# Eight half-MiB loads more, a branch on all counts, and free banks for the last scatter

## The chip, the cores and the metric

The kernel runs on one core of a Trainium2 chip. The metric is device time in microseconds (us), the median of several executions. A profile was taken of one more execution; all times of single instructions come from it, counted from the start of its span.

## The reference

A trunk of two layers on 256 tokens of width 1024. Each layer has a mixer (a gated delta rule and a sparse attention) and a feed-forward part: the first layer's is dense, the second's has eight experts, of which every token goes to two. What the change touches is the second one:

```python
def moe_ffn(h, w_router, w1, w3, w2):
    logits = (h @ w_router).astype(jnp.float32)
    top_val, top_idx = lax.top_k(logits, TOP_K)
    top_w = jax.nn.softmax(top_val, -1)
    combine = jnp.sum(jax.nn.one_hot(top_idx, N_EXPERTS, dtype=jnp.float32) * top_w[..., None], -2)
    out = jnp.zeros_like(h)
    for e in range(N_EXPERTS):
        out = out + combine[..., e:e + 1].astype(h.dtype) * swiglu(h, w1[e], w3[e], w2[e])
    return out
```

All is fp32. An expert's w1 and w3 are 1024 x 3584, its w2 is 3584 x 1024: 42 MiB an expert, 336 MiB for the eight.

## The kernel before

**Router.** After the second mixer the logits `lg` are ranked on VectorE (DVE), `sel` marks each token's two experts, and TensorE (PE) sums `sel` into the bank `pk` (line 1145): places of the tokens in their experts and, in columns 16 to 23, the number of tokens of each expert. `cnt0` (1151) is expert 0's count as an integer; `slot` (1153) is each token's place.

**Large and small experts.** An expert is computed by `Large` with 128 slots for tokens, or by `Small` with 64. `Large` splits each weight block into two parts of fp32r, hi on ScalarE (ACT) and lo on DVE (`split`, 216; rows of it stand under lines 233 and 235), and multiplies three times. The parts' tiles are `hi` and `lo` of the pool `spl` (three each) and `hi2` and `lo2` of the stage's own pool (one each), of 1072 columns. `Small` multiplies the fp32 blocks as they are, without parts, two 64-column halves side by side. Both run four groups of columns (`GRP`): `up` for w1 and w3, `mid` for silu and the transposes, `down` for w2 into the bank `py`, and at the end `scatter`, which brings the result back to the tokens and adds it to `acc` (1360).

**Gather.** `gathered` (1156) multiplies tokens with a one-hot matrix of the slots into one bank `pg`; eight DVE instructions (1165) take two such banks out. Banks named by `mi` come from the pair with the tag `pj`, which `pk`, `pg`, `put`, `pot` and `pso` share. A bank passes on to a new name when the last instruction that uses the old one is done. `hidden` (1139) hands out the four banks of the tags `dn` and `no`.

**Loads.** Weights come in 1 MiB loads, issued by SP (SyncE) in `fetch` (1214), into a ring of 14 tiles that earlier stages have used (1347). Before the branch the first 14 loads of expert 0 are issued (`loaded`, 1389 to 1395); `blocks` (1206) takes those first and then fetches further ones, each when its ring tile has been read.

**Order and branch.** From the router to `manual.close()` (1387) PE and DVE run in the order of the code. The planner orders the rest. Then every engine loads `cnt0` into a register (1493) and branches (1494): with over 64 tokens for expert 0 it runs `experts(False, ...)`, else `experts(True, ...)`. In `experts` expert 0 comes first, the others sorted by count so that large and small ones alternate: seven places, of which those from `SMALL` = 4 on are small. In the branch of 64 slots the order is small, large, small, large, large, small, large, small. `rest` works out this order, the weights and `gf2`.

**After the branch**, every engine loads `cnti`, the greatest count (of the small ones, 64 more), and branches (1501, 1502): over 128, a loop over all experts computes the tokens that found no slot, and stores the result again. `store` (1367) writes `acc`, four blocks of 256 KB: those of the first 128 tokens from ACT's queue, of the others from SP's.

Of the kernel before, what the change touches and what calls it, by code (L numbers as in the profile page):

```python
# [16 lines left out]
P = 128  # L17
# [69 lines left out]
def trunk(ctx, tc, A, out, dbg=None, stop=None):  # L87
# [39 lines left out]
    def bc(ap, shape):  # L127
        return ap.to_broadcast(shape)
# [973 lines left out]
    def moe(mp, lg, rf, px, am, manual):  # L1102
# [7 lines left out]
        eq = T([P, NT, 8, 8], "eq", bufs=2, tag="u")  # L1110
        own, other = bc(lg[:, :, :, None], [P, NT, 8, 8]), bc(lg[:, :, None, :], [P, NT, 8, 8])
# [27 lines left out]
        def hidden():  # L1139

            seq["ph"] = seq.get("ph", -1) + 1
            return bank(("dn", "dn", "dn", "no")[seq["ph"] % 4], "ph")
# [8 lines left out]
        cnt0 = T([P, 1], "cnt0", I32)  # L1151
        V.tensor_copy(cnt0, pk[:, 16:17])
# [53 lines left out]
        def blocks(w, e, r0, n, c0, width, get):  # L1206

            per = 2048 // width
            for i in range(0, n, per):
                r = loaded.pop(0) if loaded else fetch(w, e, r0 + i * P, per, c0, width, get)  # L1210
                for j in range(per):
                    yield r[:, j]

        def fetch(w, e, a, per, c0, width, get):
            r = get().rearrange("p (k n) -> p k n", k=per)
            nc.sync.dma_start(r, w[bass.ds(e, 1), a:a + per * P, c0:c0 + width].rearrange("e (k p) n -> p (e k) n", p=P))
            return r
# [66 lines left out]
        class Small:  # L1284
# [44 lines left out]
            def scatter(self, t, onet, fin):  # L1329
# [4 lines left out]
                po = [mi("pso") for n in range(2)]  # L1334
# [32 lines left out]
        def store(t, d):  # L1367
            (nc.sync if t else nc.scalar).dma_start(o_[:, t, d], acc[:, t, d])
# [9 lines left out]
        cp = T([P, NT, 7], "cp")  # L1378
        cnt = T([P, 8], "cnt")
        oneh = one_hot(slot[:, :, 0])  # L1380
# [5 lines left out]
        V.tensor_copy(cnt, pk[:, 16:24])  # L1386
# [69 lines left out]
        def experts(first, PLACE):  # L1456

            kinds = [first] + [place >= SMALL for place in PLACE]
            oneh = one_hot(slot[:, :, 0], first)
# [29 lines left out]
            for n in range(2):  # L1489
                prev.scatter(n, onet, add_to(weight(NE - 1), store))  # L1490

        was, had = dict(seq), list(loaded)
        few0 = nc.values_load(cnt0[0:1, 0:1], min_val=0, max_val=S)
        with tc.If(few0 > 64) as branch:
            experts(False, (4, 0, 1, 5, 2, 3, 6))
        with branch.Else():
            seq.update(was)
            loaded[:] = had
            experts(True, (0, 4, 1, 2, 5, 3, 6))

        mx = nc.values_load(cnti[0:1, 0:1], min_val=0, max_val=S + 64)
        with tc.If(mx > P):
            with tc.For_i(0, NE, 1) as ev:
                es_ = T([P, NT], "es")
                ec = T([P, NT], "ec")
                V.tensor_copy(es_, late_[:, :, bass.ds(ev, 1)].rearrange("p t o -> p (t o)"))
                V.tensor_copy(ec, comb[:, :, bass.ds(ev, 1)].rearrange("p t o -> p (t o)"))
                oneh = one_hot(es_)
                g = gather(oneh)
                onet = turned(oneh)  # L1510
                ex = Large(ev, g, lambda: raws.tile([P, 2048], F32, tag="raw", name="ro", bufs=RAWS))
                for q in range(4):
                    ex.up(q)
                    ex.mid(q)
                    ex.down(q)
                for n in range(2):
                    ex.scatter(n, onet, add_to(lambda t: ec[:, t:t + 1]))
            for n in range(2):
                for t in range(NT):
                    store(t, slice(n * 512, n * 512 + 512))  # L1520
# [133 lines left out]
```

## Time and profile before

| | us |
|---|---|
| median of 3 runs | 1749.4 |
| lowest and highest run | 1748.41, 1754.7 |
| the profiled execution | 1749.47 |
| its span | 1747.5 |

| engine | busy us | share of the span |
|---|---|---|
| PE, matmuls | 1659.9 | 95% |
| PEld, weight loads of PE | 1290.0 | 74% |
| DVE | 1164.2 | 67% |
| ACT | 831.7 | 48% |
| POOL | 56.9 | 3% |

The chain of work that ended last is PE for 85% of the span, DMA for 6%, DVE for 5%. Matmuls are pipelined, so that a busy PE is not PE at its peak, and an average over the span mixes stages with different limits. The stage with the eight experts runs from about 882 us to the end; its rows are to be read by themselves.

### The profile page before, as it was taken

What the parts mean: (1) busy time and instruction counts of PE and PEld (TensorE: products, weight loads), DVE (VectorE), ACT (ScalarE), POOL (GpSimd) and SP (SyncE); (2) the same over time, 40 slices, a digit from 0 to 9 for tenths busy, and PEclk for the clock granted to TensorE, in tenths of its full rate; (3) what the DMA queues carried; (4) which work ended last, traced back from release to release, by engine and by line L of the source; (5) the groups of instructions that cost most, each with busy time, mean ns of one, the idle gap of its engine ahead of it and who ended that gap; (6) DMA issues with size and microseconds to landing.
All of it is one profiled execution on the core that took longest, in us unless ns stands there. A gap on an engine that the chain in (4) does not pass through costs nothing.

```text
span 1747.5 us, 28930 instructions
## 1 busy us (share of the span) xinstructions
PE 1659.9 (95%) x11230; PEld 1290.0 (74%) x11230; DVE 1164.2 (67%) x2106; ACT 831.7 (48%) x1240; POOL 56.9 (3%) x112
## 2 busy tenths in 40 slices
PE   6997999899999999899999999999999999999997
PEld 4896878899999898788844688347887873478732
DVE  6769857799996677855521888118899971288611
ACT  3664544444444565554410676007777750277500
POOL 4400000100000200000100000000000000000000
PEclk8898979999999899999999999999999999999999
DMA  9564535599985334235679999999999999999997
GB/s 338 160 207 161 178 74 209 202 359 323 329 306 165 109 120 149 80 92 217 237 294 403 409 405 407 409 403 409 404 407 405 377 349 394 403 409 403 409 408 270
DMA packets 206431, 515.22 MB, mean 295 GB/s; under 512 B 18926, under 2 KB 58422, under 8 KB 206278
## 3 DMA queue, kind: packets, MB, share of 16 engines
q1 hardware_dynamic: 196870, 509.25, 78.2%
q10 hardware_dynamic: 9312, 3.90, 0.9%
q8 instruction: 92, 1.51, 0.3%
q14 instruction: 61, 0.50, 0.1%
q0 software_dynamic: 96, 0.07, 0.0%
HBM read 512.13 MB, written 1.05 MB: 294 GB/s over the span
## 4 chain that ended last, share of the span: by engine, by line
PE 85%; DMA 6%; DVE 5%; ACT 2%; issue 1%; SPq 0%; ACTq 0%; DVEq 0%
PE ph L1236 17%; PE ph L1299 10%; PE py L1267 9%; PE pj L239 8%; PE pj L240 8%; PE pj L241 8%; DMA m<-in_w_moe_dram 4%; PE py L1326 3%; PE py L241 2%; PE py L239 2%; PE py L240 2%; PE pSs L893 1%; PE put L125 1%; PE pn L370 1%; DMA xT<-in_w_moe_dram 1%
## 5 line engine op out<-in xcount | busy, mean ns | idle before, releaser
L235 DVE TENSOR_TENSOR wml<-m,wmh 128x1024 fp32r<-128x1024 f32 (+1 forms) x240 | 248.7, 1079 | 26.9 <-ACT wmh L233 15.5
L233 ACT ACTIVATE wmh<-m 128x1024 fp32r<-128x1024 f32 (+1 forms) x240 | 218.4, 944 | 56.2 <-DMA m<-in_w_moe_dram 20.3
L1309 DVE TENSOR_TENSOR u<-u,ph 128x512 f32<-128x512 f32 (+1 forms) x16 | 9.9, 621 | 208.4 <-PE ph L1299 208.4
L1236 PE MATMUL ph<-wmh,gh 128*128 128x512 f32 x448 | 145.4, 394 | 2.2 <-ACT wmh L233 2.2
L1236 PE MATMUL ph<-wml,gh 128*128 128x512 f32 x448 | 145.9, 396 | 1.1 <-DVE wml L235 1.0
L1236 PE MATMUL ph<-wmh,gl 128*128 128x512 f32 x448 | 145.4, 394 | 0.0
L1299 PE MATMUL ph<-m,gs 128*64 128x512 f32 (+1 forms) x720 | 139.5, 538 | 2.1 <-DMA m<-in_w_moe_dram 2.1
L239 PE MATMUL pj<-hf0h,wh 128*128 128x256 f32 x448 | 126.5, 284 | 1.2 <-ACT hf0h L341 1.2
L240 PE MATMUL pj<-hf0l,wh 128*128 128x256 f32 x448 | 126.2, 283 | 0.0
L241 PE MATMUL pj<-hf0h,wl 128*128 128x256 f32 x448 | 125.2, 283 | 0.0
L233 ACT ACTIVATE w2h<-m 128x1024 fp32r<-128x1024 f32 x104 | 107.9, 1057 | 34.8 <-PE py L1267 23.2
L235 DVE TENSOR_TENSOR w2l<-m,w2h 128x1024 fp32r<-128x1024 f32 x104 | 121.9, 1220 | 2.6 <-ACT w2h L233 2.5
L1267 PE MATMUL py<-w2h,uu 128*128 128x512 f32 x448 | 121.8, 393 | 0.0
L260 DVE SCALAR_TENSOR_TENSOR adacc<-ada,cact,adacc 128x512 f32<-128x512 f32 x158 | 117.1, 757 | 3.1 <-DMA ada<-in_w_ada_dram 2.2
L1299 PEld LDWEIGHTS ph<-m,gs 128*64 128x64 f32 x720 | 50.3, 137 | 83.3 <-issue 69.9
L233 ACT ACTIVATE wh<-win 128x1024 fp32r<-128x1024 f32 x64 | 67.4, 1057 | 78.0 <-PE pj L240 60.7
L233 ACT ACTIVATE wh<-w 128x1024 fp32r<-128x1024 f32 x56 | 59.4, 1061 | 94.4 <-PE pj L240 57.9
L1236 PEld LDWEIGHTS ph<-wml,gh 128*128 128x128 f32 x448 | 82.7, 188 | 28.0 <-DVE wml L235 7.6
L1236 PEld LDWEIGHTS ph<-wmh,gh 128*128 128x128 f32 x448 | 83.8, 188 | 24.2 <-ACT wmh L233 4.8
L1267 PEld LDWEIGHTS py<-w2h,uu 128*128 128x128 f32 x448 | 84.2, 188 | 19.6
L1236 PEld LDWEIGHTS ph<-wmh,gl 128*128 128x128 f32 x448 | 84.0, 188 | 19.5
L1326 PE MATMUL py<-m,us 128*64 128x512 f32 x416 | 94.9, 597 | 1.5 <-DMA m<-in_w_moe_dram 1.5
(650 smaller groups left out, 3939.5 us busy)
## 6 DMA issues: line engine op xcount, KB each, us to landing
m<-in_w_moe_dram SPq DMA_DIRECT2D x312, 1024.0 KB, 17.4
ada<-in_w_ada_dram SPq DMA_DIRECT2D x48, 1024.0 KB, 7.6
w<-in_w_dense_dram SPq DMA_DIRECT2D x42, 1024.0 KB, 6.8
win<-in_w_in_dram SPq DMA_DIRECT2D x34, 1024.0 KB, 5.2
xT<-in_w_moe_dram SPq DMA_DIRECT2D x24, 1024.0 KB, 17.5
wout<-in_w_out_dram SPq DMA_DIRECT2D x8, 1024.0 KB, 6.3
win<-in_w_in_dram SPq DMA_DIRECT2D x8, 536.0 KB, 3.7
win<-in_w_in_dram SPq DMA_DIRECT2D x8, 528.0 KB, 3.6
```

Source lines behind the costliest of these rows:

```text
L125: return nc.tensor.transpose(out_, in_, ident[:k, :k])
L233: SC.activation(hi, src, AF.Copy)
L235: cur["last"] = eng.tensor_tensor(lo, src, hi.bitcast(F32), op=OP.subtract).ins
L239: mm(o, w[0], x[0], start=start, stop=False, skip_group_check=True)
L240: mm(o, w[0], x[1], start=False, stop=False, skip_group_check=True)
L241: mm(o, w[1], x[0], start=False, stop=stop, skip_group_check=True)
L260: V.scalar_tensor_tensor(acc, w(k), cact[:, k:k + 1], acc, op0=OP.mult, op1=OP.add)
L370: mm(o, x[0][:, kt, s], hi[:, k], start=kt == 0, stop=False)
L1236: mm(p_, s_[:, k], d_[:, i * 512:i * 512 + 512], start=k == 0 and d_ is hi and s_ is gh, stop=k == KT - 1 and d_ is lo)
L1267: mm(p_, s_[:, j], d_[:, n * 512:n * 512 + 512], start=q + j == 0 and d_ is hi and s_ is uh, stop=q == 3 and j == nb - 1 and d_ is lo)
L1299: mm(p_[i * 64:i * 64 + 64, 0:h], self.g[k], raw[:, i * h:i * h + h], start=k == 0, stop=k == KT - 1, skip_group_check=True)
L1326: mm(self.py[n * 64:n * 64 + 64], self.u[q][:, b, i * 64:i * 64 + 64], raw[:, n * 512:n * 512 + 512], start=q + j == 0, stop=q == 3 and j ...
```

## The change

- After `before`'s constants a row `most` is set on POOL: 64 for expert 0, 128 for the others. `cnt0` goes. Between `one_hot` and the first `gathered`, DVE copies the counts out of `pk` (`cnt`, before at line 1386), and with five more instructions makes `need`: 8 for every count over `most`, 1 for every count over 64, summed, and cast to `needi`.
- The branch asks for `needi` over 4 instead of `cnt0` over 64. The loop for left over tokens stands in that branch alone, as `left_over`; the branch of 64 slots has none.
- In the branch of 64 slots eight more loads of half a MiB are fetched ahead, into `hi` and `lo` of both pools: the last four blocks of w3 of the second group and the first four of w2. `fetch` now returns with a load how many blocks it holds, and `blocks` counts by it. The ring's loads behind them are four fewer.
- The last expert's second `scatter` takes banks from `hidden` instead of `mi`. `store` sends the blocks with equal halves of tokens and columns from SP, the two others from ACT.

```diff
+        most = T([P, 8], "most")
+        G.memset(most, 128.0)
+        G.memset(most[:, 0:1], 64.0)
...
-        cnt0 = T([P, 1], "cnt0", I32)
-        V.tensor_copy(cnt0, pk[:, 16:17])
...
         def blocks(w, e, r0, n, c0, width, get):
 
-            per = 2048 // width
-            for i in range(0, n, per):
-                r = loaded.pop(0) if loaded else fetch(w, e, r0 + i * P, per, c0, width, get)
-                for j in range(per):
+            i = 0
+            while i < n:
+                m, r = loaded.pop(0) if loaded else fetch(w, e, r0 + i * P, 2048 // width, c0, width, get)
+                for j in range(m):
                     yield r[:, j]
+                i += m
...
-            def scatter(self, t, onet, fin):
+            def scatter(self, t, onet, fin, last=False):
...
-                po = [mi("pso") for n in range(2)]
+                po = [hidden() if last else mi("pso") for n in range(2)]
...
         def store(t, d):
-            (nc.sync if t else nc.scalar).dma_start(o_[:, t, d], acc[:, t, d])
+            (nc.sync if t == d.start // 512 else nc.scalar).dma_start(o_[:, t, d], acc[:, t, d])
...
-        cnt = T([P, 8], "cnt")
-        oneh = one_hot(slot[:, :, 0])
+        oneh = one_hot(slot[:, :, 0])
+        cnt = T([P, 8], "cnt")
+        over = [T([P, 8], f"over{i}") for i in range(2)]
+        need = T([P, 1], "need")
+        needi = T([P, 1], "needi", I32)
+        V.tensor_copy(cnt, pk[:, 16:24])
+        V.tensor_tensor(over[0], cnt, most, op=OP.is_gt)
+        V.tensor_scalar(over[1], cnt, 64.0, None, op0=OP.is_gt)
+        V.scalar_tensor_tensor(over[0], over[0], 8.0, over[1], op0=OP.mult, op1=OP.add)
+        V.tensor_reduce(need, over[0], axis=AX.X, op=OP.add)
+        V.tensor_copy(needi, need)
...
         gathered(oneh, 0, g0k[0:4])
         gathered(oneh, 1, g0k[4:8])
-        V.tensor_copy(cnt, pk[:, 16:24])
         manual.close()
...
         def experts(first, PLACE):
 
             kinds = [first] + [place >= SMALL for place in PLACE]
+            if first:
+
+                more = [(spl, t, SPL) for t in ("hi", "lo") * SPL] + [(mp, t, SPLM) for t in ("hi2", "lo2") * SPLM]
+                blk = [(w, i * P, GRP[1]) for w in (W1, W3) for i in range(KT)][2 * (len(loaded) - KT):]
+                blk += [(W2, i * P, (0, D)) for i in range(KT)]
+                for (pl_, tag, n), (w, a, (c0, width)) in zip(more, blk):
+                    loaded.append(fetch(w, 0, a, 1, c0, width, lambda: pl_.tile([P, 1072], F32, tag=tag, name="half", bufs=n)[:, 0:1024]))
...
-                prev.scatter(n, onet, add_to(weight(NE - 1), store))
+                prev.scatter(n, onet, add_to(weight(NE - 1), store), last=n == 1)
...
-        few0 = nc.values_load(cnt0[0:1, 0:1], min_val=0, max_val=S)
-        with tc.If(few0 > 64) as branch:
+        many = nc.values_load(needi[0:1, 0:1], min_val=0, max_val=72)
+        with tc.If(many > 4) as branch:
             experts(False, (4, 0, 1, 5, 2, 3, 6))
+            left_over()
         with branch.Else():
             seq.update(was)
             loaded[:] = had
             experts(True, (0, 4, 1, 2, 5, 3, 6))
```

`left_over` is the former block behind the branch, with the ring's tiles for its loads.

## Rows read from the trace of the kernel before

**Rows 1.** The page, part 2: GB/s of the DMA engines, 40 slices of 43.7 us.

```profile
GB/s 338 160 207 161 178 74 209 202 359 323 329 306 165 109 120 149 80 92 217 237 294 403 409 405 407 409 403 409 404 407 405 377 349 394 403 409 403 409 408 270
```

**Rows 2.** Instructions in order of time, SP, 862 to 892: start, us, engine, line, operation.

```profile
869.82 0.37 SPq L1216 DMA_DIRECT2D xT<-in_w_moe_dram  x1
884.27 7.24 SPq L1216 DMA_DIRECT2D m<-in_w_moe_dram  x5
```

**Rows 3.** Stretches: us, busy of PE, PEld, DVE, ACT, POOL, granted clock, DMA share, GB/s.

```profile
874.00:876.00 2.00, 1.52 (x9) 1.23 (x7) 0.43 (x2) 0.20 (x1) 0.00 (x0) 0.56 0.13 47
876.00:884.00 8.00, 5.45 (x24) 4.23 (x26) 2.37 (x8) 1.05 (x2) 0.00 (x0) 0.68 0.03 9
884.00:892.00 8.00, 8.00 (x40) 3.28 (x38) 4.96 (x45) 2.08 (x3) 0.00 (x0) 1.00 0.84 264
```

**Rows 4.** Waits of SP's queue, 870 to 890: us in total, times, longest.

```profile
SPq L1216 <- PE ph L1299: 12.1, 4, 8.3
```

**Rows 5.** Instructions in order of time, DVE, 862 to 892; in brackets idle time before it.

```profile
867.32 0.16 DVE L143 SCALAR_TENSOR_TENSOR hf1ry<-hf1ru,hf1ry 128x2 f32<-128x2 f32 x1
867.51 0.16 DVE L144 TENSOR_TENSOR hf1ru<-hf1ry 128x2 f32<-128x2 f32 x1
...
872.25 0.16 DVE L1152 CAST cnt<-pk 128x1 int32<-128x1 f32 x1 [1.44 <-PE pk L1150]
...
872.52 0.48 DVE L1127 TENSOR_SCALAR oneh<-ct,slot 128x128 f32<-128x128 f32 x2
875.57 1.37 DVE L1165 TENSOR_SCALAR g<-pg,am,modc 128x128 f32<-128x128 f32 x4 [2.56 <-PE pg L1162]
...
882.16 0.15 DVE L1386 COPY cnt<-pk 128x8 f32<-128x8 f32 x1
```

**Rows 6.** Instructions in order of time, PE, 862 to 892.

```profile
877.08 3.75 PE L1162 MATMUL pg<-oneh,xr 128*128 128x128 f32 x16 [1.55 <-ACT gf L1452]
882.31 4.51 PE L1299 MATMUL ph<-m,g 128*64 128x512 f32 x20 [1.48 <-issue]
```

**Rows 7.** Line 1494, the branch: ns min/median/max, first and last start.

```profile
L1494 PEldq COMPARE_BRANCH  x1: 3889/3889/3889, 878.3 to 878.3; - x1
```

**Rows 8.** The chain that ended last, in order of time: start, us, what.

```profile
931.83 32.34 DMA m<-in_w_moe_dram x2
...
966.56 23.87 PE ph L1236 x102
...
1150.02 31.69 DMA m<-in_w_moe_dram x2
...
1184.10 23.87 PE ph L1236 x102
```

**Rows 9.** Instructions in order of time, PE: the last w2 load of S0 and S2.

```profile
962.28 1.89 PE L1326 MATMUL py<-xT,us 128*64 128x512 f32 x8
...
1179.84 1.89 PE L1326 MATMUL py<-xT,us 128*64 128x512 f32 x8
```

**Rows 10.** Waits, 1092 to 1184: us in total, times, longest.

```profile
PE ph L1299 <- DMA m<-in_w_moe_dram: 2.1, 3, 0.9
```

**Rows 11.** Line 1368, the stores: ns min/median/max, first and last start; landing.

```profile
L1368 SPq DMA_DIRECT2D out_dram<-acc x2: 375/800/1225, 1740.2 to 1740.8; - x2
DMA to landing us min/median/max: 2.1/3.0/3.1
```

**Rows 12.** Line 1502, the branch behind the experts, on SP.

```profile
L1502 SPq EVENT_SEMAPHORE  x8: 17/17/17, 1745.4 to 1746.0; - x8
L1502 SPq COMPARE_BRANCH  x1: 53/53/53, 1742.7 to 1742.7; - x1
```

**Rows 13.** Instructions in order of time, DVE, 1728 to 1750: the last two additions.

```profile
1739.39 1.41 DVE L1360 SCALAR_TENSOR_TENSOR acc<-pso,cp,acc 128x512 f32<-128x512 f32 x2 [0.56 <-PE pso L1337]
```

**Rows 14.** The page, part 6: loads, count, KB each, us from issue to landing.

```profile
m<-in_w_moe_dram SPq DMA_DIRECT2D x312, 1024.0 KB, 17.4
...
win<-in_w_in_dram SPq DMA_DIRECT2D x8, 528.0 KB, 3.6
```

More of the change, by code (lines that the diff above doesn't have):

```diff
@@ L1216, in fetch @@
             nc.sync.dma_start(r, w[bass.ds(e, 1), a:a + per * P, c0:c0 + width].rearrange("e (k p) n -> p (e k) n", p=P))
-            return r
+            return per, r
         class Large:
@@ L1489, in experts, with left_over @@
             for n in range(2):
-                prev.scatter(n, onet, add_to(weight(NE - 1), store))
+                prev.scatter(n, onet, add_to(weight(NE - 1), store), last=n == 1)
+        def left_over():
+            mx = nc.values_load(cnti[0:1, 0:1], min_val=0, max_val=S + 64)
+            with tc.If(mx > P):
+                with tc.For_i(0, NE, 1) as ev:
+                    es_ = T([P, NT], "es")
+                    ec = T([P, NT], "ec")
+                    V.tensor_copy(es_, late_[:, :, bass.ds(ev, 1)].rearrange("p t o -> p (t o)"))
+                    V.tensor_copy(ec, comb[:, :, bass.ds(ev, 1)].rearrange("p t o -> p (t o)"))
+                    oneh = one_hot(es_)
+                    g = gather(oneh)
+                    onet = turned(oneh)
+                    ex = Large(ev, g, tiles)
+                    for q in range(4):
+                        ex.up(q)
+                        ex.mid(q)
+                        ex.down(q)
+                    for n in range(2):
+                        ex.scatter(n, onet, add_to(lambda t: ec[:, t:t + 1]))
+                for n in range(2):
+                    for t in range(NT):
+                        store(t, slice(n * 512, n * 512 + 512))
         was, had = dict(seq), list(loaded)
-        few0 = nc.values_load(cnt0[0:1, 0:1], min_val=0, max_val=S)
-        with tc.If(few0 > 64) as branch:
+        many = nc.values_load(needi[0:1, 0:1], min_val=0, max_val=72)
+        with tc.If(many > 4) as branch:
             experts(False, (4, 0, 1, 5, 2, 3, 6))
+            left_over()
         with branch.Else():
@@ L1499, in moe @@
             experts(True, (0, 4, 1, 2, 5, 3, 6))
[L1501 to L1520, printed above, removed]
     cur["tmp"] = ini
```

## The prediction

> **What bounds the kernel now.** I read the slices of the page first: from about 885 us to the end the DMA engines move some 403 to 409 GB/s, but for two slices near 1360 to 1440 [rows 1]. So the expert stage (0.35 GB of weights) is bound by its stream of weights as much as by TensorE, and the chain of waits says where which of the two is late. It has two long pieces in which work waits for a load: one lands at 964.17, as the second expert starts, one at 1181.71, as the fourth does; behind each PE runs without a break [rows 8]. The experts run small, large, small, large, large, small, large, small (S0, L1, S2, L3, L4, S5, L6, S7), a small one 64 slots wide.
>
> The edit aims at the start of that stream. SP issues the last of the 14 ring loads at 869.82 and the next at 884.27 [rows 2]; the DMA engines move 9 GB/s between 876 and 884 [rows 3]. SP stood inside the branch all that time: its wait for the first ring tile to come free lasted 8.3 us [rows 4], from 875.97, which is 3.56 us after the cast of `cnt0` had ended at 872.41 [rows 5].
>
> I count against the profiled execution: 1749.47 us, span 1747.5, so some 2.0 us lie outside. The median of the three runs is 1749.4; the forecast is the profiled time less the sum.
>
> **Which branch runs.** At the end SP branches past the left over tokens [rows 12], so in this data no count is over its expert's room: at most four of experts 1 to 7 have over 64 tokens, and expert 0 has no more, as the 64-column matmuls of its branch show [rows 6]. The new test (`need` over 4) takes the same branch.
>
> **The extra loads, SP's side.** `cnt0` goes, and the branch now waits for `needi`, behind the one-hot and six small operations. On DVE: `slot` from 872.25 (0.16), two one-hots 0.48, then five dependent steps, one each 0.20 (a step of such a chain, 867.32 to 867.51) [rows 5]; the sixth runs beside another. `needi` is ready near 873.95, SP is in the branch 3.56 later, at 877.5, and issues near 877.6 where it issued at 884.27. DVE has 2.56 us idle there before the first evacuation at 875.57 [rows 5], so these 1.0 us cost DVE nothing; had it no such gap, they would delay the second half of the gather by as much.
>
> How fast a stream starts: before, 264 GB/s over 884 to 892 are 2.11 MB, which is a stream at 409 GB/s since 886.84, 2.57 us after its issue. The 1 MiB load of 869.82 had 0.09 MB left at 874 [rows 3], so it ended at 874.23 and ran as if from 871.67, 1.85 after its issue. By these two the new stream counts from 879.45 to 880.2, 6.65 to 7.4 us earlier; I take 7.1. The eight halves are 4.19 MB, 10.3 us, so they last to about 890, and the ring's next loads are issued from 884.3 at the latest: no hole. Eight issues of about 0.4 us each hold SP for some 4 us, ahead of ring tiles that are not free yet. The halves lie in the parts' tiles, which L1 needs first at 964; as MiB 15 to 18 of S0's 42 they are read in its first half.
>
> **PE's side, which decides how much arrives.** S0 ends on PE at 964.17 (962.28 + 1.89) [rows 9], just when L1's first load lands: S0 is bound by PE nearly to its end. So an earlier stream gains only what PE now loses. At L1's start PE loses 1.46 us: from 964.17 to 966.56 it has but 4 matmuls of 0.23 [rows 8, 9], since a load is first split on ScalarE and VectorE. In S2 it waits 2.1 us for loads [rows 10], and at L3's start 1.44 once more (1181.73 to 1184.10) [rows 8, 9]. These are 5.0 us.
>
> To them comes an earlier start of S0, which the diff doesn't name. Before, the counts were copied out of `pk`'s bank only at 882.16, so the second gather had to use the first one's bank: it waited 1.55 us, until its evacuation ended at 876.94 [rows 5, 6]. With the counts read early, `pk`'s bank should be free, and the second gather follows at 875.53, ending at 879.28. PE's branch took 3.89 us from 878.3 [rows 7]; it can now begin once `needi` is loaded, near 874.6, and end at 878.5. S0 then starts near 879.4 instead of 882.31, 2.9 earlier. The granted clock was 0.50 to 0.56 in part of that stretch (0.68 over 876 to 884) [rows 3]; if it stays at the 1.2 GHz level to the same moment, that costs some 0.8. I take 2.5, between 0 (the bank is not handed over) and 2.9.
>
> So PE can gain up to 7.5 us, the stream 7.1. Step by step: PE is 4.0 earlier in L1, 6.1 after S2, and then the loads' 7.1 is reached, with part of L3's start still waited for. **L3 starts 7.1 us earlier** (5.0 if S0 starts as before, 7.5 at best). Behind it L3 and L4 are PE's, the ring fills and the stream drops to 377 and 349 GB/s [rows 1]: from there it is paced by tiles that PE frees, so both keep the shift, and the surplus of a lead is lost, not the shift.
>
> **The tail.** The last scatter waits for a bank: DVE sits 0.56 us idle before the last two additions [rows 13]. In free banks this goes, and the last addition ends at 1740.24. Then SP's two stores, issued behind each other (the second issue took 1.225), land by 1743.9 (1740.8 + 3.1) [rows 11]; but SP branches at 1742.7 and goes on only at 1745.4 [rows 12]. So the branch is last, not the store. It goes; the last store, now alone on SP, is issued at 1740.27 and lands 2.1 to 3.1 later [rows 11], by 1742.4 to 1743.4. If the eight semaphore steps (0.6) stay, and the 1.5 us to the end of the span, the span ends between 1744.0 and 1745.5: 2.0 to 3.5 earlier, I take 2.6. The left over test itself costs this branch nothing more, since its load and its branch stand in the other branch alone.
>
> **Sum:** 7.1 + 2.6 = 9.7 us, so 1739.8 us (0.55% faster). With the ends of both, 7.0 (5.0 + 2.0) to 11.0 (7.5 + 3.5): 1738.5 to 1742.5.
>
> **Rivals.**
> *S0 starts no earlier.* The bank isn't handed over, or PE's and DVE's code fetches for the branch now meet the running stream. For it: no row shows that bank free. Then 5.0 + 2.6 = 7.6, 1741.9 us. It is the lower part of the forecast's mechanism, with its own chance.
> *The loads come late.* SP works in order; if an extra load must wait for a tile that is still read, the ring's loads queue behind it, and the stream starts as before, near 884. Then what PE gains at S0 is waited for again at L1 and only the tail is left: 2.6, about 1746.9 us. Against it: in the code the last readers of the parts' tiles are the output projection's splits, ahead of the router.
> *Half-size loads are slow (slower).* A half-MiB load alone lands 3.6 us after its issue in the first mixer's stage [rows 14]. If eight of them ran one after the other, they would take 28.8 us from 877.6, to 906.4. Before, the stream had moved 4 MiB by 897.1 (886.84 + 10.25). L1 and L3 would start about 9 us later, and with the tail's 2.6 the time is some 1756 us. It turns slower than before once the eight take over 22 us, 2.75 each. Against it: 1 MiB loads land 17.4 us after their issue [rows 14] while the stream runs at 409 GB/s, so many are in flight at once, and SP can issue these without a wait. The Trainium skill, DMA: Bandwidth & Descriptors, section Bandwidth, says to batch to 1 MiB or more, and gives about 2.0 us fixed per transfer; by its fit, an estimate, the eight take 25.6 us if nothing overlaps, and the time would be near 1753.
>
> **How the numbers follow.** About 0.5% (8.7 us, under 1740.7) is what a measurement tells from no change. Forecast 0.62, three quarters of it beyond 0.5%; S0 no earlier 0.17, a quarter beyond; a faster ramp and an earlier S0 together (1737 to 1738.5) 0.05; loads late 0.08; half loads slow 0.03, a third of it over 1758; what I haven't named, such as another order of the branch's instructions, 0.05, split over all three. That gives faster 0.57, same 0.40, slower 0.03. A range from 1737.0 to 1744.0 holds the forecast, S0 no earlier and the faster case.
>
> **What would show it.** SP's first load of the branch near 877.6, and 380 to 410 GB/s already over 880 to 892. The second gather without idle time before it, and S0's first matmul near 879 to 880. L1's first matmul right behind S0's last. L3's start near 1174 to 1175. DVE without idle time between the last four additions, no branch on SP behind the last store, the span's end 4 to 5 us behind the last addition, where it was 6.7. I am wrong if the first extra load is issued later than 880, if S0 starts after 882.3, or if the shift at L3's start is gone at S7.

## The result

| | us |
|---|---|
| before, median (10 executions, 1748.41 to 1754.7) | 1750.1 |
| after, median (10 executions, 1738.23 to 1747.38) | 1742.03 |
| ratio, with its 95% interval | 0.9946 (0.9933 to 0.9959) |
| profiled execution of after, its span | 1741.45, 1739.7 |

The changed kernel is 9.4 us faster by the ratio (7.2 to 11.7), 8.1 by the two medians. Executions of one kernel spread over 6 to 9 us, and the longer ones show the lower mean granted clock: of the ten of the changed kernel the seven from 1738.23 to 1742.92 had 0.970 to 0.974, the three from 1745.67 up 0.966 to 0.968.

The stage ahead of the experts doesn't end at the same moment in each execution: the last load ahead of the branch is issued at 869.82 in the profile of before and at 871.59 in that of after (868.8 to 874.1 over the fourteen profiles of this text), though nothing ahead of it is changed but two settings of POOL. So I count from that load in each profile. The span ends 877.69 behind it before, 868.08 after: 9.6 us less.

SP's instructions of after, in order of time (start, us, engine, line, operation):

```profile
871.59 0.37 SPq L1218 DMA_DIRECT2D xT<-in_w_moe_dram  x1
879.69 5.39 SPq L1218 DMA_DIRECT2D half<-in_w_moe_dram  x8
885.18 4.22 SPq L1218 DMA_DIRECT2D m<-in_w_moe_dram  x4
```

The first load of the branch comes 8.1 behind the last one ahead of it; it was 14.5 [rows 2]. The 8.3 us of waiting for the first ring tile [rows 4] are gone. The eight issues take 5.39 us; by line 1218 the halves land 3.8 to 9.3 us after their issue. Stretches of after (us, busy time of PE, PEld, DVE, ACT, POOL, granted clock, DMA share, GB/s), 8 us each from the same distances as the last two of [rows 3]:

```profile
877.77:885.77 8.00, 5.40 (x29) 2.50 (x29) 4.72 (x36) 1.67 (x4) 0.00 (x0) 1.00 0.65 196
885.77:893.77 8.00, 8.00 (x40) 3.27 (x38) 1.97 (x17) 1.67 (x2) 0.00 (x0) 1.00 1.02 410
```

They were 9 and 264 GB/s. DVE and then PE of after in order of time, in brackets idle time and what ended it:

```profile
874.63 0.16 DVE L1388 COPY cnt<-pk 128x8 f32<-128x8 f32 x1
...
875.58 0.15 DVE L1393 CAST needi<-need 128x1 int32<-128x1 f32 x1
```

```profile
874.66 3.86 PE L1163 MATMUL pg<-oneh,xr 128*128 128x128 f32 x32 [0.68 <-DVE oneh L1130]
881.12 3.23 PE L1301 MATMUL ph<-m,g 128*64 128x512 f32 x14 [2.60 <-SPq L1672]
```

The counts are read behind the one-hots, so `pk`'s bank is free early. Both halves of the gather are one row of 32 matmuls: the idle 1.55 between them [rows 6] is gone. S0 starts 9.53 behind the last load, 12.49 before: 2.96 earlier. S0 doesn't wait for the gather, which ends at 878.52, but for PE's own branch, which ends at 880.96 (line 1536: ns min/median/max, first and last start); SP's semaphore, which the row names, had come at 879.6:

```profile
L1536 PEldq COMPARE_BRANCH  x1: 3406/3406/3406, 877.5 to 877.5; - x1
```

What PE waits for from the gather to the end, in part (us in total, times, longest):

```profile
PE py L1328 <- DMA m<-in_w_moe_dram: 2.7, 5, 0.7
PE ph L1301 <- SPq L1672: 2.6, 1, 2.6
PE ph L1238 <- DVE wml L235: 1.8, 3, 0.8
...
PE ph L1238 <- ACT wmh L233: 1.1, 1, 1.1
...
PE ph L1301 <- DMA m<-in_w_moe_dram: 0.2, 1, 0.2
```

S2's 2.1 us [rows 10] are gone: all waits for loads in this list, 2.9 us, lie in S7. There the kernel before has 2.0:

```profile
PE py L1326 <- DMA m<-in_w_moe_dram: 1.5, 3, 0.7
...
PE py L1326 <- DMA xT<-in_w_moe_dram: 0.5, 1, 0.5
```

The chain that ended last, at L1's and L3's start, answers to [rows 8]:

```profile
962.67 1.23 DVE wml L235
963.94 23.94 PE ph L1238 x102
...
1153.62 4.62 PE ph L1301 x43
1158.24 18.40 DMA m<-in_w_moe_dram
1176.66 1.07 ACT wmh L233
1177.75 1.24 DVE wml L235
1179.03 21.15 PE ph L1238 x90
```

Ahead of L1 no load stands in the chain any more. Ahead of L3 one does, a load of 18.40 us, issued at 1158.24 behind PE's matmuls; before, two loads of 31.69 us together stood there. The tail, DVE and then the stores of line 1370:

```profile
1731.92 0.69 DVE L1335 TENSOR_TENSOR yh<-py,gf 128x512 f32<-128x512 f32 x1 [14.82 <-PE py L1328]
1733.82 1.41 DVE L1362 SCALAR_TENSOR_TENSOR acc<-pso,cp,acc 128x512 f32<-128x512 f32 x2 [1.22 <-PE pso L1339]
1735.15 1.40 DVE L1362 SCALAR_TENSOR_TENSOR acc<-ph,cp,acc 128x512 f32<-128x512 f32 x2
```

```profile
L1370 SPq DMA_DIRECT2D out_dram<-acc x2: 356/360/365, 1734.6 to 1736.6; - x2
...
DMA to landing us min/median/max: 2.1/2.1/2.1
```

The additions follow each other without idle time, all stores land after 2.1 us, and the span ends 3.1 us behind the last addition (1736.55), where it was 6.7.

Below, a table of all profiles: the moments in us behind the last load ahead of the branch (starts, but for the two ends), each from the trace as one start less the other. "Tail" is the end less the start of the last `yh`, S7 that start less L6's last hi matmul of its `up`.

| kernel | SP's first load | S0 | L1 | L3 | L6's up ends | last yh | end | S7 | tail |
|---|---|---|---|---|---|---|---|---|---|
| before | 14.46 | 12.49 | 95.48 | 313.02 | 759.57 | 865.70 | 877.69 | 106.1 | 11.99 |
| before, second profile | 14.23 | 12.26 | 94.43 | 312.50 | 759.03 | 864.13 | 875.88 | 105.1 | 11.75 |
| tail alone | 16.27 | 14.30 | 97.60 | 315.14 | 761.69 | 867.69 | 875.69 | 106.0 | 8.00 |
| after | 8.10 | 9.53 | 90.36 | 306.18 | 752.87 | 860.32 | 868.08 | 107.4 | 7.76 |
| after, second profile | 7.86 | 9.45 | 90.27 | 305.81 | 752.49 | 859.36 | 867.12 | 106.9 | 7.76 |
| stores' queues back | 7.98 | 9.59 | 90.41 | 306.31 | 753.00 | 858.51 | 866.28 | 105.5 | 7.77 |
| branch at the end | 7.91 | 11.15 | 91.97 | 306.79 | 753.82 | 859.27 | 870.33 | 105.5 | 11.06 |
| scatter's old banks | 8.24 | 11.03 | 91.86 | 307.76 | 754.46 | 859.08 | 868.35 | 104.6 | 9.26 |
| two halves | 7.97 | 9.45 | 89.97 | 307.23 | 753.76 | 859.74 | 867.70 | 106.0 | 7.96 |
| no halves | 11.61 | 9.64 | 92.82 | 310.39 | 757.04 | 863.41 | 871.41 | 106.4 | 8.01 |
| counts' bank held | 7.84 | 12.11 | 96.27 | 310.70 | 758.17 | 863.83 | 871.59 | 105.7 | 7.76 |
| the same, 32 bytes more | 7.93 | 11.83 | 94.46 | 309.38 | 758.18 | 864.24 | 872.00 | 106.1 | 7.76 |
| test ahead of one-hots | 7.79 | 14.12 | 97.79 | 312.22 | 759.66 | 865.30 | 873.06 | 105.6 | 7.76 |
| six matmuls more | 8.51 | 10.45 | 93.33 | 307.76 | 755.22 | 861.29 | 869.05 | 106.1 | 7.76 |

### The profile page after: what moved, and what is told of

Same layout as the page of the kernel before. It is cut to its first block, busy times and chain, and to the rows that moved or that the text cites. A ratio compares the mean times of both kernels' runs of the same rounds, so it can differ in the third digit from the quotient of the medians.

```text
span 1739.7 us, 28944 instructions
## 1 busy us (share of the span) xinstructions
PE 1657.6 (95%) x11230; PEld 1288.6 (74%) x11230; DVE 1164.7 (67%) x2110; ACT 832.2 (48%) x1240; POOL 57.5 (3%) x114
## 5 line engine op out<-in xcount | busy, mean ns | idle before, releaser
L235 DVE TENSOR_TENSOR wml<-m,wmh 128x1024 fp32r<-128x1024 f32 (+1 forms) x248 | 257.8, 1085 | 26.9 <-ACT wmh L233 21.3
L233 ACT ACTIVATE wmh<-m 128x1024 fp32r<-128x1024 f32 (+1 forms) x248 | 226.4, 947 | 56.3 <-PE ph L1238 25.0
L1301 PE MATMUL ph<-m,gs 128*64 128x512 f32 (+1 forms) x744 | 144.4, 540 | 0.2 <-DMA m<-in_w_moe_dram 0.2
L233 ACT ACTIVATE w2h<-m 128x1024 fp32r<-128x1024 f32 x96 | 100.3, 1057 | 31.7 <-PE py L1269 23.5
L235 DVE TENSOR_TENSOR w2l<-m,w2h 128x1024 fp32r<-128x1024 f32 x96 | 112.7, 1223 | 1.0 <-ACT w2h L233 1.0
L1328 PE MATMUL py<-m,us 128*64 128x512 f32 x376 | 87.2, 598 | 2.7 <-DMA m<-in_w_moe_dram 2.7
```

The lines of the kernel that those rows point to most:

```text
L233: SC.activation(hi, src, AF.Copy)
L235: cur["last"] = eng.tensor_tensor(lo, src, hi.bitcast(F32), op=OP.subtract).ins
L1301: mm(p_[i * 64:i * 64 + 64, 0:h], self.g[k], raw[:, i * h:i * h + h], start=k == 0, stop=k == KT - 1, skip_group_check=True)
L1328: mm(self.py[n * 64:n * 64 + 64], self.u[q][:, b, i * 64:i * 64 + 64], raw[:, n * 512:n * 512 + 512], start=q + j == 0, stop=q == 3 and j ...
```

## The experiments

A ratio is to the kernel before, measured beside the run. Where none is given, there was one execution, the profiled one.

**The changed kernel once more.** No edit.

> The changed kernel once more, for a second profile of it. Counted from the last load ahead of the branch (to leave out how long the front of the kernel took), the first profile ended 868.1 us later, where the kernel before took 877.7. If the 1.4 us by which the loads' lead fell in S5 to S7 (from 6.8 to 5.4) belongs to the kernel, this profile shows it at the same place and ends within 0.5 us of 868.1. If it is chance, S7 keeps a lead of 6.7 to 6.9 and the end comes near 866.7. The ratio to the kernel before should be near 0.9946 either way.

Ratio 0.9924 (0.9900 to 0.9949). Up to the end of L6 the profile is the first one within 0.4 us. S7 takes 106.9 us, 107.4 in the first. The seven profiles of kernels whose S7 is that of the changed kernel or of before ("after" and "before" twice each, "stores' queues back", "branch at the end", "scatter's old banks") lie between 104.6 and 107.4, without order by their edits. They do go with what PE waits for loads in S7: 0.9 us at 104.6 ("scatter's old banks"), 1.2 at 105.1 (the second of before), 2.0 at 106.1 (the first), 2.6 at 106.9 and 2.9 at 107.4 (the changed kernel). At the end of S7 PE works 1.94 us on a load of w2 and then sits idle until the next lands, as here in the first profile of after:

```profile
1724.84 1.94 PE L1328 MATMUL py<-m,us 128*64 128x512 f32 x8 [0.61 <-DMA m<-in_w_moe_dram]
```

So of the 1.3 us that the first profile's lead lost in S7, 0.9 are waits for loads: the stream is late there once more. S7 of one kernel differs by 1.0 between two profiles (before) and by 0.5 (after), so a part is chance; how large a part, these runs don't tell.

**No halves.**

```diff
-                for (pl_, tag, n), (w, a, (c0, width)) in zip(more, blk):
+                for (pl_, tag, n), (w, a, (c0, width)) in zip(more[:0], blk):
```

> The eight half-MiB loads go; the early counts, the new test and the tail stay. If the body's gain is the stream's earlier start by whatever load comes first: the branch's first ring load still waits for the tile that the second gather reads, which now ends near 878.5 where it ended at 880.8, so the stream starts 2 to 3 us earlier than in the kernel before, S0 still starts some 2.9 us earlier, L3 starts 2 to 3 us earlier, and with the tail's 4.2 the sum is 6 to 7 us (ratio 0.9960 to 0.9966). If all of the body's gain is the halves' alone, L3 starts as before and only the tail's 4.2 is left (ratio 0.9976).

Ratio 0.9953 (0.9939 to 0.9968); the profile ends 6.3 us earlier than before's. SP:

```profile
872.26 0.37 SPq L1218 DMA_DIRECT2D xT<-in_w_moe_dram  x1
883.87 16.35 SPq L1218 DMA_DIRECT2D m<-in_w_moe_dram  x10
```

The first theory holds: S0, the first load, L1 and L3 all come 2.6 to 2.9 us earlier. What the halves add to that shows beside it: the seven executions of this kernel took 1742.57 to 1746.98, the four of the changed kernel in the same series 1737.96 to 1742.54, and L3 starts 4.2 to 4.6 us earlier with them. One detail of the expectation was wrong: the ring tile comes free not with the gather but with S0's first matmuls, 2 us into S0 (11.61 less 9.64), as before (14.46 less 12.49). Without the halves the stream hangs on S0's start.

**Two halves.**

```diff
-                for (pl_, tag, n), (w, a, (c0, width)) in zip(more, blk):
+                for (pl_, tag, n), (w, a, (c0, width)) in zip(more[:2], blk):
```

> Two halves in place of eight. If what counts is when the stream starts: two halves are issued near 877.9 and 878.6 (counted from the last load ahead of the branch as in the kernel before) and last 2.5 us, the ring's first tile comes free at 879 to 881 and its loads follow without a hole, so that L3 starts 6 to 6.9 us earlier, as with eight, and the ratio is that of the changed kernel within 0.0005 (0.9946). If what counts is the bytes that lie outside the ring: 1 MiB instead of 4, a quarter of 6.85, 1.7 us, or 2.9 with S0's start, and the ratio is near 0.9963 to 0.9968.

Ratio 0.9934 (0.9908 to 0.9960). SP:

```profile
879.21 1.25 SPq L1218 DMA_DIRECT2D half<-in_w_moe_dram  x2
882.65 16.34 SPq L1218 DMA_DIRECT2D m<-in_w_moe_dram  x10
```

L3 starts 5.8 us earlier than before, a little under the 6 to 6.9 of the first theory and far from the 2.9 of the second. Between the second half's issue and the first ring load 2.2 us pass, and L3 is 1 us later than with eight. So most of the gain is when the stream starts; the other six halves, which lie outside the ring as well, bring 1.0 of 6.8 us at L3. By the ratio the two kernels can't be told apart.

**The counts' bank held.** Both kernels copy the counts a second time behind the gather; the first into a tile of its own ("the same, 32 bytes more" in the table), the second into `cnt` ("counts' bank held").

```diff
         gathered(oneh, 1, g0k[4:8])
+        V.tensor_copy(T([P, 8], "held"), pk[:, 16:24])
```

> The counts are copied early as in the changed kernel, and once more behind the second gather, into a tile that nothing reads, which holds their bank as before the change. My theory of S0's start: the second gather then waits again for the first one's evacuation (1.5 us idle), the granted clock falls to 0.5 to 0.6 again, S0 starts near 882 where it starts at 879.4 in the changed kernel (counted from the last load ahead of the branch). The stream still starts 6.85 earlier; L1 starts only some 2 us earlier (5.1 in the changed kernel), what PE lacks is 2 to 3 us up to L3, and the end comes 1 to 2.5 us later than the changed kernel's. Rival: S0's start only shifts waiting from one place to the other, since S2's wait for loads (2.1) and L3's take it up; then the end moves by less than 0.5.

```diff
         gathered(oneh, 1, g0k[4:8])
+        V.tensor_copy(cnt, pk[:, 16:24])
```

> Like the run that held the counts' bank through a second copy, but the second copy goes into the counts' own tile, so that no other tile of SBUF moves. That run lost two things: 2.4 us at S0's start with the counts' bank, and then a drift of 1.3 us between L3's start and the end of L6, in steps of 0.01 us on the experts' matmuls (the same instructions, each some 0.3% longer). If the drift came with the 32 bytes by which the extra tile moved the others, it is gone here: S0 0.7 earlier than in the kernel before (counted from the last load ahead of the branch), L3 2.8 to 3.6 earlier, and L6's end still as much, with the end some 7 us earlier than before where the changed kernel has 9.6 to 10.5. If the drift is of another origin, L6's end has lost 1 to 1.5 of L3's lead again. In both cases the PE side is confirmed as the limit up to L3 if L3's lead is 3 to 4 with the first load of the branch 6.4 to 6.6 earlier.

Ratios 0.9999 (0.9983 to 1.0014) and 0.9967 (0.9953 to 0.9981). PE of the second, in order of time, and a stretch of the first:

```profile
875.51 2.02 PE L1163 MATMUL pg<-oneh,xr 128*128 128x128 f32 x16 [0.68 <-DVE oneh L1130]
879.09 2.02 PE L1163 MATMUL pg<-oneh,xr 128*128 128x128 f32 x16 [1.55 <-DVE g L1166]
884.55 7.49 PE L1301 MATMUL ph<-m,g 128*64 128x512 f32 x20 [3.44 <-issue]
```

```profile
880.00:885.50 5.50, 3.42 (x10) 1.27 (x12) 1.62 (x13) 0.00 (x0) 0.00 (x0) 0.69 0.99 364
```

The 1.55 between the halves is back, as [rows 6] had it, and S0 starts 2.3 to 2.7 later than in the changed kernel. The granted clock falls too, but behind the gather and into S0: in the second, 20 matmuls take 7.49 us that took 4.51 in [rows 6]. With SP's first load as early as in the changed kernel, L3 is only 3.6 and 2.3 earlier than before at its first matmul, and L4 2.4 and 1.5. From L1 to L3 PE waits for no load in either. So **PE decides here what arrives at L3**, and S0's earlier start is as much a condition of the gain as the loads are. How much of the loss is the bank's wait and how much the clock's fall behind it, these two don't separate.

There is a drift too: between L3 and the end of L6 the kernel with the tile of its own loses 1.3 us more than the one without. Rows of matmuls of each (count, busy time, mean ns), the first kernel and then the second:

```profile
L1238 PE MATMUL ph<-wmh,gh 128*128 128x512 f32 x448 | 145.8, 395 | 0.0
...
L1269 PE MATMUL py<-w2h,uu 128*128 128x512 f32 x448 | 122.8, 396 | 0.0
```

```profile
L1238 PE MATMUL ph<-wmh,gh 128*128 128x512 f32 x448 | 145.3, 393 | 0.0
L1269 PE MATMUL py<-w2h,uu 128*128 128x512 f32 x448 | 122.0, 394 | 0.0
```

In this one profile of each, a part of the matmuls start 0.01 us further apart. The extra tile of 32 bytes is the only difference between the two kernels, but no view shows where the tiles lie, and the cause stays open.

The distance between the two ratios isn't explained by these profiles. That of the first is of its shortest execution, 1744.06: two more took 1746.36 and 1747.72, all three at a mean granted clock of 0.971 to 0.974, and the other seven 1752.13 to 1754.37 at 0.964 to 0.969. Of the second, eight took 1742.72 to 1749.10 at 0.969 to 0.972, two 1749.79 and 1751.61 at 0.965. So the distance goes with the clock that the executions were granted; why the first has more of the low ones, no run shows.

**The test ahead of the one-hots.**

```diff
-        oneh = one_hot(slot[:, :, 0])
         cnt = T([P, 8], "cnt")
...
         V.tensor_copy(needi, need)
+        oneh = one_hot(slot[:, :, 0])
```

> The test's six small operations go ahead of the one-hots, so the test's value is ready 0.4 us earlier (the one-hots' 0.40) and the gather starts 1.1 later (five steps of 0.20 and one beside). SP's first load then comes 0.4 earlier (7.5 after the last load ahead of the branch, where the changed kernel has 7.9 to 8.1), and S0 starts 1.1 later (10.6 where it has 9.5). Theory that PE limits the lead up to L3: L1 and L3 start 0.5 to 1.1 later than in the changed kernel, in spite of the earlier stream, and the end 0.3 to 1.1 later. Rival, that the stream alone decides: L3 starts 0.4 earlier and so does the end.

Ratio 0.9944 (0.9922 to 0.9966), that of the changed kernel. Its profile says little of the two theories: the execution was the longest of its four (1748.37; the others 1740.75 to 1745.68), with the granted clock at 0.50 and 0.55 in two stretches. SP's load came 0.1 to 0.3 earlier where 0.4 was expected, the gather 1.0 later (1.1), but S0 4.6 later where 1.1 was. Inconclusive.

```profile
877.00:881.00 4.00, 3.51 (x16) 3.54 (x17) 0.54 (x3) 0.07 (x1) 0.00 (x0) 0.50 0.24 91
...
889.00:893.00 4.00, 4.00 (x12) 1.24 (x10) 2.37 (x22) 0.00 (x0) 0.00 (x0) 0.55 1.02 402
```

**The branch at the end.** `left_over()` is called behind both branches, as before.

```diff
             experts(False, (4, 0, 1, 5, 2, 3, 6))
-            left_over()
         with branch.Else():
...
             experts(True, (0, 4, 1, 2, 5, 3, 6))
+        left_over()
```

> The left over tokens' test goes back behind both branches, all else as changed. Theory: SP meets its branch behind the last store (issued 2.6 us after the last addition's start), which takes 2.7 us, then the eight semaphore steps (0.6) and 1.5 to the end: from the start of the last yh to the end 10.1 to 10.6 us, where the changed kernel has 7.8 and the kernel before 12.0. The branch is then 2.3 to 2.8 of the tail's 4.2. Rival: the branch runs beside the last store's landing and costs at most 0.8.

The tail is 11.06 us, 3.3 more than the changed kernel's and over the 10.1 to 10.6 of the theory. Line 1514, the branch, and line 1370, the stores:

```profile
L1514 SPq EVENT_SEMAPHORE  x8: 17/17/17, 1741.8 to 1742.3; - x8
...
L1370 SPq DMA_DIRECT2D out_dram<-acc x2: 356/360/364, 1735.5 to 1737.5; - x2
...
DMA to landing us min/median/max: 2.3/3.1/3.8
```

SP issues its last store at 1737.52, loads the count, branches at 1738.85, goes on at 1741.80 and is through the eight semaphore steps of line 1514 at 1742.4. From the count's load at 1737.93 these are 4.5 us; in the changed kernel SP waits 1.3 us in that place for the stores to land. The stores' landing takes 2.3 to 3.8 with the branch running beside them, 2.1 without. The rival (0.8) falls.

The same profile shows something else. Its gather and its branch are those of the changed kernel, yet S0 starts 1.6 us later, because the granted clock dips. PE, and a stretch from the gather's start on:

```profile
876.75 6.58 PE L1163 MATMUL pg<-oneh,xr 128*128 128x128 f32 x32 [0.68 <-DVE oneh L1130]
884.74 4.51 PE L1301 MATMUL ph<-m,g 128*64 128x512 f32 x20 [1.40 <-DVE cols L1166]
```

```profile
876.60:880.60 4.00, 3.85 (x18) 3.88 (x19) 1.06 (x9) 0.00 (x0) 0.00 (x0) 0.50 0.39 155
```

The second profile of the changed kernel, in the same place:

```profile
872.10:876.10 4.00, 3.81 (x32) 3.64 (x32) 2.38 (x12) 0.00 (x0) 0.00 (x0) 1.00 0.37 144
```

With the clock at its 1.2 GHz level (granted 0.50) in those 4 us the same 32 matmuls take 6.58 us instead of 3.81, S0 starts 1.6 later, and L3 0.6 to 1.0 (1.6 to 2.0 in the next profile, which has the same dip).

**The scatter's old banks.**

```diff
-                prev.scatter(n, onet, add_to(weight(NE - 1), store), last=n == 1)
+                prev.scatter(n, onet, add_to(weight(NE - 1), store), last=False)
```

> The last scatter goes back to the two banks of the one before, all else as changed. Theory: 0.5 to 0.6 us of idle time of VectorE come back ahead of the last two additions, and the end comes as much later: 8.3 to 8.4 us from the start of the last yh to the end, where the changed kernel has 7.8. Rival: the wait is covered by the stores (the first store's landing), and the tail stays 7.8.

The tail is 9.26, 1.5 more: more than the 0.5 to 0.6 of the theory, and the rival (nothing) falls. DVE, and a stretch:

```profile
1737.58 0.75 DVE L1362 SCALAR_TENSOR_TENSOR acc<-pso,cp,acc 128x512 f32<-128x512 f32 x1 [1.05 <-PE pso L1339]
1738.70 0.75 DVE L1362 SCALAR_TENSOR_TENSOR acc<-pso,cp,acc 128x512 f32<-128x512 f32 x1 [0.36 <-PE pso L1339]
```

```profile
1736.00:1740.00 4.00, 2.66 (x4) 0.72 (x4) 2.04 (x3) 0.00 (x0) 0.00 (x0) 0.55 0.52 197
```

The idle time is 1.41 where [rows 13] has 0.56. In both kernels the last scatter waits 0.84 us for its bank, but its four matmuls took 2.73 us here, at the lower clock, and 1.78 in both profiles of before, at 1.00. So of the 1.5 us some 0.6 are the bank's and some 0.9 this execution's clock; whether the bank's wait brings the clock down with it, one profile doesn't tell. The clock fell around the gather in this execution too (S0 at 11.03).

**The stores' queues back.**

```diff
-            (nc.sync if t == d.start // 512 else nc.scalar).dma_start(o_[:, t, d], acc[:, t, d])
+            (nc.sync if t else nc.scalar).dma_start(o_[:, t, d], acc[:, t, d])
```

> The stores' queues go back (both stores of the second half of the rows on SP, the others on ScalarE), all else as changed: the last two stores share SP's queue again. In the kernel before the second of them took 1.23 us to issue, against 0.36 to 0.37 in the changed kernel, and landed 3.1 after its issue, against 2.1. Theory, by those rows: the tail (start of the last yh to the end) grows by 0.9 to 1.9, from 7.8 to 8.7 to 9.7. Rival, by what the other two runs left of the tail's 4.2 (3.3 for the branch, 0.56 for the bank): 0.3 to 0.4 only, so 8.1 to 8.2, because the slow issue in the kernel before came from something else than the shared queue. A third thing read from it: whether the granted clock falls around the gather in this execution, with the same code there as in the changed kernel.

```profile
L1370 SPq DMA_DIRECT2D out_dram<-acc x2: 356/360/364, 1733.9 to 1734.6; - x2
```

The tail is 7.77, the same. The second issue on the shared queue takes 0.36 as well. Both theories fall: the shared queue alone brings neither the 1.225 nor the landing of 3.1 in [rows 11]. The slow landing goes with the branch: the three profiles with a branch behind the stores (before twice, "branch at the end") have 3.1 to 3.8 at most, the eleven without 2.0 to 2.2. The slow issue is in the second profile of before as well, on line 1368:

```profile
L1368 SPq DMA_DIRECT2D out_dram<-acc x2: 371/786/1200, 1740.1 to 1740.8; - x2
```

"Branch at the end" has the branch without the shared queue and issues in 0.36. So the slow issue was seen only where queue and branch come together; the changed kernel with both wasn't run, and its cause stays open.

**The tail alone.** The kernel before, with the three edits of the tail.

```diff
+                po = [hidden() if last else mi("pso") for n in range(2)]
...
+            (nc.sync if t == d.start // 512 else nc.scalar).dma_start(o_[:, t, d], acc[:, t, d])
...
             experts(False, (4, 0, 1, 5, 2, 3, 6))
+            left_over()
...
```

> The kernel before with the changed kernel's tail alone: the last scatter in free banks, the stores' queues, and the left over tokens' test inside the other branch; no early counts, no extra loads. Theory: the tail (from the start of the last yh to the end) is 7.8 us as in the changed kernel, where the kernel before has 12.0, and nothing else moves: a gain of 4.2 us, ratio 0.9976. If the branch at the end was worth only the 2.6 of my sum, the tail is 9.4 and the ratio 0.9985.

Ratio 0.9981 (0.9969 to 0.9993), 3.3 us; tail 8.00, 4.0 less than before's. The interval holds both expectations, the profile only the first. But "nothing else moves" was wrong for this execution: the gather stood 0.4 later and S0 1.8.

**The kernel before once more.** No edit.

> The kernel before once more, for a second profile. In the two profiles of the changed kernel the granted clock stayed 1.00 around the gather and S0 started 9.5 after the last load ahead of the branch; in two later ones with the same code there it fell to 0.50 from 876 to 883 and S0 started at 11.0 to 11.2. So part of what I read as the change's gain at S0 may be the clock's state in one execution. If the dip belongs to the kernel before (its gather stands idle 1.55 us between its halves), this profile shows it again, S0 starts near 12.5 and the end comes near 877.7 after that load. If it is chance here too, a profile without it shows S0 at 10.5 to 11.5 and an end near 876.

The dip is there again, and so is S0 near 12.3. The end, though, comes at 875.88 and not near 877.7: 0.5 us of the 1.8 are there at the end of L6, 1.0 is S7, 0.2 the tail. Against this profile the second one of the changed kernel ends 8.8 earlier, where the two first ones are 9.6 apart. The gather's stretch:

```profile
874.40:878.40 4.00, 2.57 (x16) 2.30 (x16) 1.44 (x5) 1.06 (x2) 0.00 (x0) 0.67 0.38 152
```

All three profiles of before's gather have it; of the five of the changed kernel's gather and branch ("after" twice, the stores' queues, the branch, the scatter) two have. "No halves" and "two halves" run the same instructions up to the branch, and neither has it: two of seven. What decides it in an execution, I can't tell from these.

**Six matmuls more.**

```diff
         pk = mi("pk")
+        for i in range(6):
+            mm(pk[:, 256:384], C["upi"], eq.rearrange("p t a b -> p (t a b)"), start=True, stop=True)
```

> The changed kernel with six matmuls of 128x128 whose result nobody reads, in TensorE's 1.2 us of idle time ahead of the routing's small matmuls (some 0.8 us of work, so they should delay nothing). Theory: the dip of the granted clock around the gather follows from how little TensorE does just ahead of it, and is what splits the changed kernel's times into a lower group (1738 to 1743) and an upper one (1745 to 1747). With the gap filled, the clock stays 1.00 from the gather to S0 in the profile, S0 starts at 9.5 to 9.7 after the last load ahead of the branch, and few or no runs lie in the upper group: a median of 1738 to 1741. Rival: the dip depends on the idle time behind the gather (the branch) or on where in the execution it falls; then the upper group stays at a quarter to a third of the runs and the median is near 1742.

Ratio 0.9942 (0.9926 to 0.9959), median 1740.56, four executions from 1739.75 to 1741.98: as the theory had it, but four are too few to tell, and the profile speaks against it. PE, and a stretch from just ahead of S0:

```profile
869.11 1.58 PE L1150 MATMUL pk<-eq,ct 128*128 128x128 f32 x12 [0.35 <-DVE eq L1117]
```

```profile
878.30:883.80 5.50, 4.52 (x14) 1.77 (x16) 3.42 (x36) 0.85 (x2) 0.00 (x0) 0.69 0.90 277
```

The six run as twelve instructions and take 1.58, not 0.8, so the gather starts 0.5 later; the clock stays up there, but falls in S0 instead, behind PE's idle time in the branch (3.08 here). The rival has that much for it. In this profile, filling one gap moved the dip and didn't remove it.

## Why the prediction was right, and where only its sum was

The forecast was 1739.8, the time is 1742.03 (by the ratio, from the 1749.4 that the forecast started from, 1740.0), inside the range. By step:

**The stream's start (7.1 us, and S0's 2.5): right.** `needi` was forecast 4.1 behind the last load, SP's first load 7.8; they came at 4.14 and 7.86 to 8.10. L3 starts 6.84, 7.21 and 6.71 earlier than in the first profile of before in three profiles without a dip (the changed kernel twice, "stores' queues back"). The second gather follows the first, and S0 is 2.9 to 3.0 earlier there, the upper end of its term; 1.34 and 1.46 where the clock fell. For that I had put 0.8; it is 1.6. S0's moment came out by luck, though: I had the gather end last, 9.46 behind the last load, and PE's branch at 8.7. In the first profile the gather ended at 6.93, since it ran at the full clock, and the branch at 9.36, since PE began it only 5.96 behind that load, where I had 4.8. So S0 waits for the branch. The halves stream at 410 GB/s, so *half-size loads are slow* falls. The Trainium skill, DMA: Bandwidth & Descriptors, gives about 2.0 us of fixed time per transfer in its section "Anatomy of one DMA — SWDGE (gpsimd) path", as a fit for transfers issued from GpSimd. Here, from SP's queue and with several in flight, the trace of after shows no such cost one behind the other: the fifth to the seventh half landed 1.27 and 1.29 us apart.

**The conversion at L1, S2 and L3: right, by its sum.** From S0's start to L1's ninth hi matmul the lead grows from 2.96 to 4.37, by 1.41 (forecast 1.46), though not as told: L1's first matmul is 5.1 earlier and then 0.8 is lost to a part that DVE still has to split. Through S2 and L3's start it grows to 6.8 (2.1 and part of 1.44). The rival *S0 starts no earlier* was put at 5.0 for the body. Where the bank was held, S0 still came 0.7 and 0.4 earlier than before, and yet the body came out at 1.4 us at the end of L6; the clock's fall in S0 is a part of that (20 matmuls in 7.49 us for 4.51). So in these two profiles that rival left less than I gave it. *The loads come late* didn't happen, and was priced too low: where no halves are loaded, the stream starts with S0, and that alone is 2.6 us of body beside the tail.

**"Both keep the shift": right to the end of L6** (6.7 of 6.84). In S7 the first profile loses 1.3, of which 0.9 are waits for loads. The forecast has no such term: it looked at what paces L3 and L4, and left out that S7 meets the stream again. What part of the 1.3 is chance stays open.

**The tail (2.6): mis-sized, 4.0 to 4.2.** The step that failed is "if the eight semaphore steps (0.6) stay, and the 1.5 us to the end of the span". They don't stay: the eight steps belong to the branch (line 1502) and go with it, and a part of the 1.5 us, SP's steps at the end of the program, now runs while the store lands. From the landing to the end it is 1.0 us (last landing 1738.7, end 1739.7). And the store lands after 2.1, the lower end of the 2.1 to 3.1; the upper was seen only with the branch. Put back alone, the branch costs 3.3 of the tail. With some 0.6 for the scatter's bank and nothing for the stores' queues, 0.1 to 0.3 of the 4.0 to 4.2 stay open.

So two sums meet by chance: in the profile, a body of 5.4 (6.7 less S7's 1.3) for the 7.1, a tail of 4.2 for the 2.6, 9.6 for the 9.7.

## What to carry to other kernels

A wait on a tile at the head of a stage tears a hole into the stream, and two small loads into idle tiles can close most of it: "two halves" got 5.8 of 6.8 us. But an earlier stream arrives only as far as the engine that eats it is earlier too; here that came from reading a bank early, an edit that looked like bookkeeping. A branch at the very end kept SP for 4.5 us here, of which 3.3 came to the tail, so test early, or in the branch that needs it. And a lead lasts only to the next stage in which the other engine is the limit: in S7 PE waited for the stream again.

## What the runs showed of the hardware that I had not expected

The granted clock around the gather is not a property of the kernel: the same instructions ran at 1.00 in five profiles and at 0.50 in two, and 32 matmuls took 3.8 to 3.9 us or 6.6. In the 3 us ahead of the gather PE was busy for 1.25 to 1.36 us in all seven. The clock fell ahead of the gather, between its halves or behind it, each time near idle time of PE, but the same idle time didn't bring it down each time. One profile of a kernel can thus put 1.6 us on the wrong account; S0's gain of 2.96 is partly the dip that all three profiles of before's gather have. No kernel tried here did measurably better than the changed one.
